# A decoder trunk on one core: low parts of the first layer's activations moved to 1280 bytes behind the high ones, raw weights in four buffers of 512 KB

## The chip, the cores and the metric

The kernel runs on one core of one Trainium2 chip. The metric is the device time of one execution in microseconds; for a single core that is the core's own time. A comparison takes the median of several runs.

## What is computed

The reference is a decoder trunk of two layers on 16 meta tokens and 256 input tokens (272 rows of 2048 features, float32). Cut to what matters:

```
h = concat(meta_tokens, x)                                    # 272 x 2048
# layer 0
q, k, v, f = split(rms_norm(h, g) @ fox_w_in)                 # 2048 x (3*2048 + 16)
h += forgetting_attention(q, k, v, cumsum(log_sigmoid(f + b))) @ fox_w_o
h += square(relu(rms_norm(h, g) @ w_up[0])) @ w_down[0]       # 2048 x 8192 x 2048
# layer 1
k, v = split(rms_norm(h, g_kv) @ w_kv)                        # 2048 x 4096
h += stick_breaking_attention(rms_norm(h, g) @ sb_w_q, k, v) @ sb_w_o
h += square(relu(rms_norm(h, g) @ w_up[1])) @ w_down[1]
return rms_norm(h, g)[16:]                                    # 256 x 2048
```

The work is in the products with the weight matrices, 384 MB of float32 in all, each read once.

## The kernel before, in words

Activations are kept feature-major: 16 chunks of 128 features on the partitions, with the tokens along the row. Every large product is made by `gemm_group` (L158): it makes 512 output features, four accumulators of 128 features, over all 16 chunks. There are 96 groups: 12 for q, k and v, 4 for the first output projection, 32 for the first MLP, 8 for the shared k and v, 4 for q of the second layer, 4 for its output projection, 32 for its MLP.

**The split.** A float32 factor is carried as a high part of type `float32r` and a low part, the rest that the high part leaves out. A product is hi x hi + hi x lo + lo x hi. For the weights the split is done in the group: a raw tile `raw` lands by DMA (L176), ACT copies it to `whi` (L185) and DVE subtracts to get `wlo` (L186), two chunks (half of a block of four chunks) at a time. For the activations a `Split` (L106) holds a tile of 16 rows, one for each chunk, with a row of `XROW` = 576 words; 16 words are left free at its head (`XHI`), then come `n` words of high part and, right behind, `n` words of low part. `n` is the number of tokens: 272 in the first layer and for the shared k and v (`t0` = 0), 256 (`S`) in the rest of the second (`t0` = 16).

**The matmuls.** With `pairs` off (n = 272) each chunk and accumulator gets three: whi with hi (L208), whi with lo (L209), wlo with hi (L210), 272 columns each. The weight is loaded anew for each. With `pairs` on (n = 256) there are two: whi with hi and lo together, 512 columns (L205), as both lie next to each other (`self.both`, L114), and wlo with hi, 256 columns (L206). The names in the profile: x_a, x_o, x_m, x_u and x_kv are `Split` tiles, so the 272-column lines with x_a are the projections q, k and v, with x_o the output projection, with x_m the up and with x_u the down products.

**Buffers.** Raw weights have three buffers of four chunks (1 MB, 8 KB in each partition), filled by one DMA each, except in the very first group, where x is loaded along with the weights and the pieces are 1, 2, 2 and 4 chunks (L172). `whi` and `wlo` have three buffers of two chunks each. Two `Split` tiles alternate.

**The order.** The program is written in the order of the groups; a scheduler with a timeline of its own reorders instructions of each engine a little and places the waits. All raw loads are issued by SP in the order of the program: a load waits until ACT and DVE have split what was in its buffer. ACT's split waits in turn until PE is done with a `whi` buffer. In a group, blocks 0 to 2 are run half by half (both chunks of a half for one accumulator after the other), block 3 accumulator by accumulator over all four chunks (L191 to L195); then each accumulator is evacuated by `evac`.

Of the kernel before, what the change touches and what calls it, by code (L numbers as in the profile page):

```python
# [9 lines left out]
F32 = mybir.dt.float32  # L10
# [5 lines left out]
P = 128  # L16
# [3 lines left out]
S = 256  # L20
# [2 lines left out]
BIG = 1.0e30  # L23
QSCALE = 1.0 / math.sqrt(P)
N_FF = 4
XROW = 576
XHI = 16

G_A0, G_M0, G_KV, G_A1, G_M1, G_FIN = range(6)

# [2 lines left out]
def yoco_kernel(ctx: ExitStack, tc: tile.TileContext, hT_in, gains, b_f, w_f, w_qkv0, w_o0, w_up, w_dn,  # L33
                w_kv, w_q1, w_o1, outT):
    nc = tc.nc

    const = ctx.enter_context(tc.tile_pool(name="const", bufs=1))
    wraw = ctx.enter_context(tc.tile_pool(name="wraw", bufs=3))

    align = ctx.enter_context(tc.tile_pool(name="align", bufs=1))  # L40
    wspl = ctx.enter_context(tc.tile_pool(name="wspl", bufs=3))
# [64 lines left out]
    class Split:  # L106


        def __init__(self, label, t0):
            n = T - t0  # L110
            self.t0 = t0
            rows = xs.tile([P, NC, XROW], F32R, tag="x", name=f"x_{label}")
            self.hi, self.lo = rows[:, :, XHI:XHI + n], rows[:, :, XHI + n:XHI + 2 * n]
            self.both = rows[:, :, XHI:XHI + 2 * n]  # L114

    def split_chunk(sp, gi, c):
# [41 lines left out]
    def gemm_group(wblk, sp, t0, evac, before={}, after={}, load_x=None, pairs=False):  # L158

        uid[0] += 1
        u = uid[0]
        accs = [pacc.tile([P, 512], F32, tag="acc", name=f"acc_{u}_{m}") for m in range(4)]
        n = T - t0
        for kb in range(4):
            raw = wraw.tile([P, 4, 512], F32, tag="raw", name=f"raw_{u}_{kb}")
            src_w = wblk[kb].rearrange("p (k c) -> p k c", k=4)
            if kb in before:  # L170
                before[kb]()
            piece = 4 if load_x is None else (1, 2, 2, 4)[kb]  # L172
            for k0 in range(0, 4, piece):
                if load_x is not None:
                    load_x(range(4 * kb + k0, 4 * kb + k0 + piece))
                nc.sync.dma_start(raw[:, k0:k0 + piece], src_w[:, k0:k0 + piece])  # L176
            piece = min(piece, 2)
            parts = []
            for hf in range(2):
                whi = wspl.tile([P, 2, 512], F32R, tag="whi", name=f"whi_{u}_{kb}_{hf}")  # L180
                wlo = wspl.tile([P, 2, 512], F32R, tag="wlo", name=f"wlo_{u}_{kb}_{hf}")
                for o in range(0, 2, piece):
                    src = raw[:, 2 * hf + o:2 * hf + o + piece, :]
                    hp, lp = whi[:, o:o + piece], wlo[:, o:o + piece]
                    on_act = nc.scalar.activation(hp, src, AF.Copy)  # L185
                    on_dve = nc.vector.tensor_tensor(out=lp, in0=src, in1=hp.bitcast(F32), op=ALU.subtract)  # L186
                parts.append((whi, wlo))
            if kb in after:
                with tc.issue_after(on_act.ins), tc.issue_after(on_dve.ins):
                    after[kb]()  # L190
            order = [(kc, m) for hf in range(2) for m in range(4) for kc in range(2 * hf, 2 * hf + 2)]  # L191
            if load_x is not None and kb == 0:
                order = [(kc, m) for kc in range(4) for m in range(4)]
            if kb == 3:
                order = [(kc, m) for m in range(4) for kc in range(4)]  # L195
            for kc, m in order:
                whi, wlo = parts[kc // 2]
                k = 4 * kb + kc
                wh = whi[:, kc % 2, m * P:(m + 1) * P]
                wl = wlo[:, kc % 2, m * P:(m + 1) * P]  # L200
                first = kb == 0 and kc == 0
                last = kb == 3 and kc == 3
                hi, lo = sp.hi[:, k], sp.lo[:, k]
                if pairs:
                    nc.tensor.matmul(accs[m], wh, sp.both[:, k], start=first, stop=False)  # L205
                    nc.tensor.matmul(accs[m][:, :n], wl, hi, start=False, stop=last)  # L206
                else:
                    nc.tensor.matmul(accs[m][:, :n], wh, hi, start=first, stop=False)  # L208
                    nc.tensor.matmul(accs[m][:, :n], wh, lo, start=False, stop=False)  # L209
                    nc.tensor.matmul(accs[m][:, :n], wl, hi, start=False, stop=last)  # L210
                if last:
                    evac(m, [accs[m][:, :n]] + ([accs[m][:, n:]] if pairs else []))
# [18 lines left out]
    def load_x(chunks):  # L231
        c0, n = chunks[0], len(chunks)
        nc.sync.dma_start(hT[:, c0:c0 + n, :], hT_in[:, c0:c0 + n, :])
        for c in chunks:
            split_chunk(xa, G_A0, c)
# [73 lines left out]
    for g in range(4):  # L309
# [11 lines left out]
        if g == 0:  # L321
            gemm_group(w_qkv0[0], xa, 0, evac_q, after={kb: (lambda kb=kb: first_norm(kb)) for kb in range(4)}, load_x=load_x)
            forget_gates(box["rstd"])
        else:
            gemm_group(w_qkv0[3 * g], xa, 0, evac_q)
# [4 lines left out]
        def decays(j):  # L330

            for i, (o, n) in enumerate(((0, 144), (144, T))):
                nc.vector.scalar_tensor_tensor(out=s[:, j, o:o + n], in0=fk[:, j, :n],
                                               scalar=fq_sb[:, i, 4 * g + j:4 * g + j + 1],
                                               in1=maskA[:, o:o + n], op0=ALU.subtract, op1=ALU.add)

        gemm_group(w_qkv0[3 * g + 1], xa, 0, lambda m, acc: evac_kv(m, acc, kT),
                   after={j: (lambda j=j: decays(j)) for j in range(4)})

# [261 lines left out]
    for b in range(2):  # L601
        nc.tensor.matmul(pr[:, b * P:(b + 1) * P], rs[:, b:b + 1].to_broadcast([P, P]), ident, start=True, stop=True)
    ob = xs.tile([P, NC, XROW], F32, tag="x", name="ob")
    for c in range(0, NC, 2):
# [54 lines left out]
```

## Time and profile before

| what | us |
|---|---|
| median of 3 runs | 2360.26 (2360.25 to 2360.53) |
| profiled execution, its own time | 2360.9 |
| span of that profile | 2359.2 |
| PE busy (matmuls) | 2340.6 |
| PEld busy (weight loads) | 2207.3 |
| DVE busy | 1343.8 |
| ACT busy | 1057.9 |
| mean granted TensorE clock | 0.998 |

The profile is one execution; its span runs from the first to the last instruction, and the execution's own time has 1.7 us around it. PE and PEld are two rows of one engine: a weight load runs beside the matmul before it, and a matmul's end is modelled and lies beyond the start of the next one. So durations of neighbours overlap, and what one matmul costs is the distance from its start to the next start. In a row of a group, `x1024 | 293.4, 289 | 0.0` means 1024 instructions, 293.4 us in which at least one of them was busy, 289 ns mean duration of one, and 0.0 us of idle time of the engine before them. In the view of one line, `284/289/289` is the minimum, median and maximum duration in ns. In a row of windows, the bounds come first, then the length, then for each engine its busy time with the count, then the clock, the DMA engines' share and GB/s.

### The profile page before, as it was taken

The numbers are of one execution on the slowest core, as the hardware profiler recorded it, in microseconds if no ns is written. First come the engines' busy times: TensorE is split into PE (matmuls) and PEld (weight loads), VectorE is DVE, ScalarE is ACT, GpSimd is POOL, SyncE is SP. The second block draws the span as 40 slices with busy tenths as digits, with TensorE's granted clock in tenths as the row PEclk, the third lists the DMA queues.
The fourth block names the chain that finished last, engine by engine and source line by source line (L and its number), as shares of the span: only waits on it lengthen the run. The fifth ranks groups of instructions, "written<-read, shape, count | busy, mean of one in ns | idle before, by whom it ended". The sixth has DMA issues, their size and how long they took to land.

```text
span 2359.2 us, 39072 instructions
## 1 busy us (share of the span) xinstructions
PE 2340.6 (99%) x16478; PEld 2207.3 (94%) x16478; DVE 1343.8 (57%) x1917; ACT 1057.9 (45%) x1473; POOL 35.2 (1%) x62
## 2 busy tenths in 40 slices
PE   8999999999999999999999999999999999999998
PEld 8999999999999999999998999988888888888887
DVE  7565555655455455445566555566555655655665
ACT  5443344543344344334445444445543543543544
POOL 0000000000000000000000000000000000000000
PEclk9999999999999999999999999999999999999999
DMA  6444444454545445544445444344545545455453
GB/s 231 147 166 171 154 160 163 176 181 168 189 163 185 173 179 179 179 179 172 179 168 197 155 147 145 143 177 180 184 177 193 194 181 197 171 188 195 178 196 125
DMA packets 60863, 411.92 MB, mean 175 GB/s; under 512 B 7040, under 2 KB 9744, under 8 KB 11920
## 3 DMA queue, kind: packets, MB, share of 16 engines
q1 hardware_dynamic: 59632, 407.05, 47.6%
q8 instruction: 129, 2.11, 0.3%
q10 hardware_dynamic: 1056, 2.38, 0.3%
q14 instruction: 46, 0.38, 0.0%
HBM read 407.29 MB, written 2.11 MB: 174 GB/s over the span
## 4 chain that ended last, share of the span: by engine, by line
PE 99%; DVE 0%; ACT 0%; DMA 0%; issue 0%; SPq 0%; DVEq 0%
PE acc L205 25%; PE acc L208 19%; PE acc L209 19%; PE acc L210 19%; PE acc L206 13%; PE ps L345 0%; PE pza L521 0%; PE pv L287 0%; PE po L406 0%; PE po L407 0%; PE po L560 0%; DVE ob L605 0%; PE po L561 0%; PE pzb L522 0%; DMA raw<-w_qkv 0%; PE po L408 0%
## 5 line engine op out<-in xcount | busy, mean ns | idle before, releaser
L186 DVE TENSOR_TENSOR wlo<-raw,whi 128x1024 fp32r<-128x1024 f32 (+1 forms) x770 | 932.0, 1220 | 764.3 <-ACT whi L185 761.2
L185 ACT ACTIVATE whi<-raw 128x1024 fp32r<-128x1024 f32 (+1 forms) x770 | 803.0, 1055 | 1071.4 <-PE acc L209 675.7
L205 PE MATMUL acc<-x_m,whi 128*128 128x512 f32 x1024 | 343.1, 394 | 0.5 <-DVE relu L223 0.5
L205 PE MATMUL acc<-x_u,whi 128*128 128x512 f32 x1024 | 343.0, 394 | 0.0
L208 PE MATMUL acc<-x_m,whi 128*128 128x272 f32 x1024 | 293.4, 289 | 0.0
L208 PE MATMUL acc<-x_u,whi 128*128 128x272 f32 x1024 | 293.2, 289 | 0.0
L209 PE MATMUL acc<-x_m,whi 128*128 128x272 f32 x1024 | 290.4, 286 | 0.0
L209 PE MATMUL acc<-x_u,whi 128*128 128x272 f32 x1024 | 290.3, 286 | 0.0
L210 PE MATMUL acc<-x_u,wlo 128*128 128x272 f32 x1024 | 280.7, 284 | 0.0
L210 PE MATMUL acc<-x_m,wlo 128*128 128x272 f32 x1024 | 280.7, 284 | 0.0
L206 PE MATMUL acc<-x_m,wlo 128*128 128x256 f32 x1024 | 252.7, 282 | 0.0
L206 PE MATMUL acc<-x_u,wlo 128*128 128x256 f32 x1024 | 251.4, 281 | 0.0
L208 PE MATMUL acc<-x_a,whi 128*128 128x272 f32 x768 | 222.9, 294 | 6.3 <-ACT whi L185 6.3
L209 PE MATMUL acc<-x_a,whi 128*128 128x272 f32 x768 | 221.9, 292 | 0.0
L205 PEld LDWEIGHTS acc<-x_u,whi 128*128 128x128 f32 x1024 | 185.4, 188 | 30.6
L205 PEld LDWEIGHTS acc<-x_m,whi 128*128 128x128 f32 x1024 | 185.0, 188 | 30.2 <-DVE relu L223 0.9
L210 PE MATMUL acc<-x_a,wlo 128*128 128x272 f32 x768 | 212.3, 288 | 0.0
L206 PEld LDWEIGHTS acc<-x_m,wlo 128*128 128x128 f32 x1024 | 192.2, 188 | 19.6 <-DVE wlo L186 4.8
L206 PEld LDWEIGHTS acc<-x_u,wlo 128*128 128x128 f32 x1024 | 192.3, 188 | 16.1 <-DVE wlo L186 1.5
L208 PEld LDWEIGHTS acc<-x_m,whi 128*128 128x128 f32 x1024 | 192.5, 188 | 0.0
L208 PEld LDWEIGHTS acc<-x_u,whi 128*128 128x128 f32 x1024 | 192.5, 188 | 0.0
L209 PEld LDWEIGHTS acc<-x_m,whi 128*128 128x128 f32 x1024 | 192.3, 188 | 0.0
(242 smaller groups left out, 3604.2 us busy)
## 6 DMA issues: line engine op xcount, KB each, us to landing
raw<-w_up SPq DMA_DIRECT2D x128, 1024.0 KB, 4.8
raw<-w_dn SPq DMA_DIRECT2D x128, 1024.0 KB, 4.8
raw<-w_qkv SPq DMA_DIRECT2D x45, 1024.0 KB, 4.7
raw<-w_o SPq DMA_DIRECT2D x32, 1024.0 KB, 4.7
raw<-w_kv SPq DMA_DIRECT2D x32, 1024.0 KB, 4.8
raw<-w_q SPq DMA_DIRECT2D x16, 1024.0 KB, 4.8
fk<-f_dram ACTq DMA_DIRECT2D x4, 544.0 KB, 5.3
raw<-w_qkv SPq DMA_DIRECT2D x4, 512.0 KB, 7.1
```

The costliest lines, as they stand in the source:

```text
L185: on_act = nc.scalar.activation(hp, src, AF.Copy)
L186: on_dve = nc.vector.tensor_tensor(out=lp, in0=src, in1=hp.bitcast(F32), op=ALU.subtract)
L205: nc.tensor.matmul(accs[m], wh, sp.both[:, k], start=first, stop=False)
L206: nc.tensor.matmul(accs[m][:, :n], wl, hi, start=False, stop=last)
L208: nc.tensor.matmul(accs[m][:, :n], wh, hi, start=first, stop=False)
L209: nc.tensor.matmul(accs[m][:, :n], wh, lo, start=False, stop=False)
L210: nc.tensor.matmul(accs[m][:, :n], wl, hi, start=False, stop=last)
```

## The change

Rows of the `Split` tiles become 640 words (2560 bytes) long. For n = 272 the low part starts at word 336 instead of word 288, which is 320 words (1280 bytes) behind the start of the high part instead of 272 words (1088 bytes); between both lie 48 unused words. For n = 256 the low part stays right behind the high part, 1024 bytes on. The two tiles need 8192 bytes a partition more.

The raw weights get four buffers of two chunks (512 KB, 4 KB in each partition) instead of three of four, 8192 bytes a partition less. Each block of four chunks is now loaded by two DMAs, one for each half, and each half has a tile of its own. In the first group the pieces are 1, 2, 2 and 2 chunks.

```diff
-XROW = 576
+XROW = 640
 XHI = 16
+XLO = 336
...
-    wraw = ctx.enter_context(tc.tile_pool(name="wraw", bufs=3))
+    wraw = ctx.enter_context(tc.tile_pool(name="wraw", bufs=4))
...
-            self.hi, self.lo = rows[:, :, XHI:XHI + n], rows[:, :, XHI + n:XHI + 2 * n]
+            lo = XHI + n if n == S else XLO
+            self.hi, self.lo = rows[:, :, XHI:XHI + n], rows[:, :, lo:lo + n]
             self.both = rows[:, :, XHI:XHI + 2 * n]
...
-            raw = wraw.tile([P, 4, 512], F32, tag="raw", name=f"raw_{u}_{kb}")
             src_w = wblk[kb].rearrange("p (k c) -> p k c", k=4)
             if kb in before:
                 before[kb]()
-            piece = 4 if load_x is None else (1, 2, 2, 4)[kb]
+            piece = 1 if load_x is not None and kb == 0 else 2
+            raws = [wraw.tile([P, 2, 512], F32, tag="raw", name=f"raw_{u}_{kb}_{hf}") for hf in range(2)]
             for k0 in range(0, 4, piece):
                 if load_x is not None:
                     load_x(range(4 * kb + k0, 4 * kb + k0 + piece))
-                nc.sync.dma_start(raw[:, k0:k0 + piece], src_w[:, k0:k0 + piece])
-            piece = min(piece, 2)
+                nc.sync.dma_start(raws[k0 // 2][:, k0 % 2:k0 % 2 + piece], src_w[:, k0:k0 + piece])
             parts = []
             for hf in range(2):
...
-                    src = raw[:, 2 * hf + o:2 * hf + o + piece, :]
+                    src = raws[hf][:, o:o + piece, :]
```

## The prediction

> **What bounds the kernel now.** I read the profile's page first, in the order span, busy engines, clock, chain of work that ended last. PE is busy for 2340.6 of 2359.2 us at a full granted clock, and PE is 99% of the chain; nearly all of that chain stands on five lines, L205, L206, L208, L209 and L210, the matmuls of `gemm_group`. So the time is a count of matmuls times their spacing, and a change counts if it alters that spacing or makes PE wait.
>
> ```profile
> span 2359.2 us, 39072 instructions
> PE 2340.6 (99%) x16478; PEld 2207.3 (94%) x16478; DVE 1343.8 (57%) x1917; ACT 1057.9 (45%) x1473; POOL 35.2 (1%) x62
> PEclk9999999999999999999999999999999999999999
> PE 99%; DVE 0%; ACT 0%; DMA 0%; issue 0%; SPq 0%; DVEq 0%
> PE acc L205 25%; PE acc L208 19%; PE acc L209 19%; PE acc L210 19%; PE acc L206 13%; PE ps L345 0%; PE pza L521 0%; PE pv L287 0%; PE po L406 0%; PE po L407 0%; PE po L560 0%; DVE ob L605 0%; PE po L561 0%; PE pzb L522 0%; DMA raw<-w_qkv 0%; PE po L408 0%
> ```
>
> Next the groups by line: the counts and the mean duration of one. The lines L208 (hi), L209 (lo), L210 (hi again, with the low part of the weight) form triples of 272 columns; L205 and L206 are the pairs of 512 and 256 columns.
>
> ```profile
> L205 PE MATMUL acc<-x_m,whi 128*128 128x512 f32 x1024 | 343.1, 394 | 0.5 <-DVE relu L223 0.5
> L208 PE MATMUL acc<-x_m,whi 128*128 128x272 f32 x1024 | 293.4, 289 | 0.0
> L208 PE MATMUL acc<-x_u,whi 128*128 128x272 f32 x1024 | 293.2, 289 | 0.0
> L206 PE MATMUL acc<-x_m,wlo 128*128 128x256 f32 x1024 | 252.7, 282 | 0.0
> L206 PE MATMUL acc<-x_u,wlo 128*128 128x256 f32 x1024 | 251.4, 281 | 0.0
> L208 PE MATMUL acc<-x_a,whi 128*128 128x272 f32 x768 | 222.9, 294 | 6.3 <-ACT whi L185 6.3
> ...
> L208 PE MATMUL acc<-x_kv,whi 128*128 128x272 f32 x512 | 146.6, 289 | 0.0
> L208 PE MATMUL acc<-x_o,whi 128*128 128x272 f32 x256 | 73.4, 289 | 0.0
> ```
>
> The triples number 1024 + 1024 + 768 + 512 + 256 = 3584. A matmul overlaps the next, so its duration is not its cost; the spacing is. Two windows count starts: 700 us of triples, then 400 us of pairs.
>
> ```profile
> 500.00:1200.00 700.00, 536.97 (x1876) 352.44 (x1875) 1.00 0.49 177
> 1900.00:2300.00 400.00, 380.13 (x1138) 205.50 (x1137) 1.00 0.51 187
> ```
>
> A triple takes 700 / 1876 = 373.1 ns, 124.4 each; a pair takes 400 / 1138 = 351.5 ns. Now the row that decides, the durations of the three lines (minimum/median/maximum):
>
> ```profile
> L208 PE MATMUL acc<-x_u,whi x1006: 284/289/289, 537.9 to 1199.8; 128*128 128x272 f32 x168
> ...
> L209 PE MATMUL acc<-x_u,whi x1006: 286/286/286, 538.0 to 1199.9; 128*128 128x272 f32 x168
> ...
> L210 PE MATMUL acc<-x_u,wlo x1005: 284/284/289, 538.1 to 1199.7; 128*128 128x272 f32 x168
> ```
>
> There are only three values. L208 and L210 read the same bytes, yet one is mostly 289 and the other mostly 284. The timeline tells which is which.
>
> ```profile
> 699.79 0.28 PE L210 MATMUL acc<-x_m,wlo 128*128 128x272 f32 x1
> 699.92 0.29 PE L208 MATMUL acc<-x_m,whi 128*128 128x272 f32 x1
> 700.04 0.29 PE L209 MATMUL acc<-x_m,whi 128*128 128x272 f32 x1
> 700.17 0.28 PE L208 MATMUL acc<-x_m,whi 128*128 128x272 f32 x1
> 700.29 0.29 PE L209 MATMUL acc<-x_m,whi 128*128 128x272 f32 x1
> 700.41 0.28 PE L210 MATMUL acc<-x_m,wlo 128*128 128x272 f32 x1
> ```
>
> L208 lasts 0.29 behind L210 (hi behind hi) and 0.28 behind L209 (hi behind lo), with L209 behind it both times; the two pairs begun by these L208 take 0.25 and 0.24 us. So a matmul's cost goes by where it and the one ahead of it start reading: hi behind hi 289, lo behind hi 286, hi behind lo 284. Their mean 286.3 less the spacing 124.4 gives 161.9 of overlap; the spacings are about 127, 124 and 122 ns.
>
> **Part one: where lo starts.** In the built program the x tiles start at a multiple of 256 bytes in both kernels, and rows of 2304 and 2560 bytes are 9 and 10 times 256. Hi starts 64 bytes behind such a multiple. Lo starts 1088 bytes on, 128 behind a multiple, before; 1280 bytes on, so 64 behind a multiple as hi does, after. The stationary tiles move by 8192 bytes and keep their residues. Hence after the change each matmul of a triple stands behind one of its own kind, which is what hi behind hi is now. I have three estimates of that spacing.
>
> First, the durations: 289 less 161.9 is 127.1; three are 381.3, 8.2 more than 373.1.
>
> Second, the start, where the first group runs equal lines in a row:
>
> ```profile
> 10.98 1.04 PE L210 MATMUL acc<-x_a,wlo 128*128 128x272 f32 x4
> 11.86 0.66 PE L208 MATMUL acc<-x_a,whi 128*128 128x272 f32 x4
> 12.35 0.55 PE L209 MATMUL acc<-x_a,whi 128*128 128x272 f32 x3
> 12.73 0.55 PE L210 MATMUL acc<-x_a,wlo 128*128 128x272 f32 x3
> 13.12 0.29 PE L209 MATMUL acc<-x_a,whi 128*128 128x272 f32 x1
> ```
>
> From 11.86 to 13.12 there are ten spacings in 1260 ns: eight of like behind like, lo behind lo among them, one lo behind hi and one hi behind lo. A triple is one of each, 373.1; so seven like ones are 1260 - 373.1 = 886.9, one is 126.7, and three are 380.1: 7.0 more.
>
> Third, the pairs, in which lo follows hi without a gap and every read starts 64 behind a multiple: durations 394 and 282, less (394 + 282 - 351.5) / 2 = 162.2, give 231.8 and 119.8. One column costs (231.8 - 119.8) / 256 = 0.4375 ns, 16 more 7.0; 272 columns would take 126.8, three of them 380.4: 7.3 more.
>
> Ends are modelled in the first and the third, and the second rests on ten matmuls rounded to 10 ns, so I take the lower side, **6.5 ns a triple**. 3584 x 6.5 = 23.3 us, all on the path, since PE waits for nothing there (idle 0.0 in the rows). Bounds: 3584 x 8.2 = 29 us above; below, nothing or a gain by the rivals.
>
> A rule of the Trainium skill speaks against any such term: "TensorE: Matmul & The Clock Gate", section "Back-to-back issue gap", gives the gap as N / 2.4 + 2.5 ns, 115.8 for 272 columns, with no word of where a read starts. The trace differs, with 124.4 on the mean and three values for one size. By the rule the term would be zero, the second rival below.
>
> The rows of the pairs are also moved, from 2304 to 2560 bytes; their starts keep their residue of 256, so I take 0. The L206 of the two tiles differ by 1 ns (282 and 281) though all else is alike; that much on the 2048 pairs of these tiles is 2 us either way.
>
> **Part two: the raw weights.** Each load of 1 MB becomes two of 512 KB in four buffers: 2 MB ahead in place of 3. SP issues 381 loads more (four in each of 95 groups, one in the first), with little else to do: it has 0% of the chain. A buffer is free when ACT (L185) and DVE (L186) have split it, so the load for half h waits for DVE's split of half h - 4 and must land before ACT's split of h. The shortest such distance in the trace is at the start of a group in the second layer:
>
> ```profile
> 1857.35 3.50 DVE L186 TENSOR_TENSOR wlo<-raw,whi 128x1024 fp32r<-128x1024 f32 x3 [1.63 <-ACT whi L185]
> ...
> 1863.45 1.06 ACT L185 ACTIVATE whi<-raw 128x1024 fp32r<-128x1024 f32 x1 [1.72 <-PE acc L205]
> ```
>
> The first of the three splits ends near 1858.57 and the split four halves on begins at 1863.45: 4.9 us. What the loads take:
>
> ```profile
> raw<-w_up SPq DMA_DIRECT2D x128, 1024.0 KB, 4.8
> raw<-w_qkv SPq DMA_DIRECT2D x4, 512.0 KB, 7.1
> ```
>
> The whole 1 MB lands in 4.8 us in the steady part, so a half of it lands in time; the 7.1 belongs to the crowded start. ACT there waits for PE, and PE has another split half in hand. I take 0. The Trainium skill speaks against it too: "SBUF — State Buffer", section "The DMA setup-cost knee", wants the largest single transfer, as each pays some 2 us. By its fit, an estimate, 512 KB take 3.2 us and 1 MB 4.4; the trace has 4.8 for the latter. This would not make the halves late.
>
> At the start the halves matter more. The load of the fourth block goes out at 12.27 before; after, its halves wait for the splits of the third and fourth half:
>
> ```profile
> 12.27 45.54 SPq L176 DMA_DIRECT2D raw<-w_qkv  x8
> ...
> 13.96 1.23 DVE L186 TENSOR_TENSOR wlo<-raw,whi 128x1024 fp32r<-128x1024 f32 x1 [0.26 <-ACT whi L185]
> ...
> 15.92 1.22 DVE L186 TENSOR_TENSOR wlo<-raw,whi 128x1024 fp32r<-128x1024 f32 x1
> ...
> 23.66 1.99 ACT L185 ACTIVATE whi<-raw 128x1024 fp32r<-128x1024 f32 x2
> ```
>
> So they go out at 15.2 and 17.1, up to 4.9 us later, and are split at 23.66, 6.5 us behind the second; the DMA engines have earlier loads to move meanwhile. I take 0, between a gain of 1 (the first half no longer waits for the second) and a loss of 4.9. The order on PE, DVE and ACT differs in a few dozen rows, nearly all in the first three groups; also 0.
>
> **Sum.** 2360.9 for the profiled execution (2359.2 of span and 1.7 around it) + 23.3 = 2384.2. The median of the three runs is 2360.3, 0.6 lower: 2383.6, a little under 1% slower.
>
> **The rivals.**
> *Like starts are what is cheap.* If hi behind hi is dear only because chunk and weight change there, and it is the different start of lo that costs, every matmul would go at the pace of hi behind lo: 122.1 ns, 3 x 122.1 = 366.3, 6.8 less, 3584 x 6.8 = 24 us faster, 2336. It decides from the point where like behind like falls below 124.4. For it: no row shows hi behind a lo with hi's start. Against it: in the run of ten, equal starts, some with the chunk unchanged, cost 126.7.
> *Only the columns count.* A pair costs 351.5 / 768 = 0.458 ns a column, a triple 373.1 / 816 = 0.457. If the durations only share out a fixed sum, nothing changes: 2360, give or take 3. Against it: the two pairs of 0.25 and 0.24 us, with equal columns.
> *The halves come late.* If a half took the 7.1 us of the start, each of the 16 up groups of the second layer would lose 7.1 - 4.9 = 2.2 us, 35 us on top of the forecast: 2419. The 4.8 us for twice the bytes speak against it.
> *It doesn't do what it says.* Another base of the tiles could undo the alignment; the built addresses exclude that.
>
> **How the numbers follow.** Forecast 0.67, late halves 0.03, columns alone 0.18, like starts cheap 0.12. Slower by over 0.2% (4.7 us, about what a measurement of this kernel can tell from no change) is 0.70, within it 0.18, faster 0.12. The range must take in the second rival, since the forecast alone is under 0.8: from 2357 to 2391, the forecast with 29 us and 2 more at the top. The forecast's own range is 2376 to 2391.
>
> **What would show it.** If right, L208, L209 and L210 all last 289 in the rows, whatever stands ahead, a window of triples gives 126.5 ns a start, L205 and L206 keep 394 and 282, and PE has no new idle time. All at 284 makes the first rival; unequal durations with 124.4 the second; idle PE behind ACT's split with a DMA named, the third. A changed time in the pairs, or a row stride that matters beyond 256 bytes, would make the prediction wrong in another way.

## The result, and the profile after

The changed kernel takes 2382.71 us (median of 4 runs, 2382.05 to 2383.3) where the kernel before takes 2360.4 beside it (4 runs, 2360.25 to 2360.92). The ratio is 1.0093, with a 95% interval of 1.008 to 1.0106: slower by 22.3 us, where 23.3 were forecast.

The page of the profile after, the lines that answer to those of before. All line numbers of `gemm_group` are one higher: L209 is hi, L210 lo, L211 wlo with hi, L206 and L207 the pairs.

```profile
span 2381.6 us, 40038 instructions
PE 2363.1 (99%) x16478; PEld 2229.9 (94%) x16478; DVE 1344.3 (56%) x1917; ACT 1057.5 (44%) x1473; POOL 33.4 (1%) x62
...
PE 99%; DVE 0%; ACT 0%; DMA 0%; issue 0%; SPq 0%; DVEq 0%
...
L206 PE MATMUL acc<-x_m,whi 128*128 128x512 f32 x1024 | 343.2, 394 | 0.5 <-DVE relu L224 0.5
...
L209 PE MATMUL acc<-x_m,whi 128*128 128x272 f32 x1024 | 293.9, 289 | 0.0
...
L210 PE MATMUL acc<-x_m,whi 128*128 128x272 f32 x1024 | 293.7, 289 | 0.0
...
L211 PE MATMUL acc<-x_m,wlo 128*128 128x272 f32 x1024 | 285.5, 289 | 0.0
L207 PE MATMUL acc<-x_m,wlo 128*128 128x256 f32 x1024 | 252.6, 282 | 0.0
```

The span grew by 22.4 us and PE's busy time by 22.5, with the same 16478 matmuls and the same clock. The pairs kept 394 and 282. The view of each line shows that the three values of before have become one:

```profile
L209 PE MATMUL acc<-x_u,whi x955: 289/289/289, 545.5 to 1199.8; 128*128 128x272 f32 x191
...
L210 PE MATMUL acc<-x_u,whi x955: 289/289/289, 545.6 to 1200.0; 128*128 128x272 f32 x191
...
L211 PE MATMUL acc<-x_u,wlo x954: 289/289/289, 545.7 to 1199.7; 128*128 128x272 f32 x191
```

Minimum, median and maximum are all 289. The two windows, triples first:

```profile
500.00:1200.00 700.00, 528.06 (x1842) 345.62 (x1841) 1.00 0.53 174
...
1900.00:2300.00 400.00, 380.05 (x1137) 205.38 (x1136) 1.00 0.56 187
```

A triple takes 700 / 1842 = 380.0 ns, 6.9 more than before; a pair 400 / 1137 = 351.8, as before (one start more or less in a window is 0.2 and 0.3 ns). PE's waits are those of before, some 10 us in all, and the loads of half the size land, by their medians, inside the 4.9 us that were needed:

```profile
PE acc L209 <- ACT whi L186: 6.4, 1, 6.4
PE pr_fin L603 <- DVE fin L600: 1.5, 1, 1.5
```

```profile
raw<-w_up SPq DMA_DIRECT2D x256, 512.0 KB, 4.5
...
raw<-w_o SPq DMA_DIRECT2D x64, 512.0 KB, 3.8
```

So the whole loss stands in the triples. Summed from each start to the next over both traces they grew by 22.3 us, which is 6.2 ns each on the mean of all 3584. It is 6.6 to 6.7 ns in the up and down groups, where the window lies (its 6.9 carries one start more or less in both counts), 6.4 in the output projection, 5.6 in the shared k and v and 5.5 in q, k and v. What was open is why, and whether it was the reason that the prediction gave: a cost for each pair of starts, with like behind like the dearest.

### The profile page after: what moved, and what is told of

Read it like the earlier page. It is cut to its first block, busy times and chain, and to the rows that moved or that the text cites. A ratio compares the mean times of both kernels' runs of the same rounds, so it can differ in the third digit from the quotient of the medians.

```text
span 2381.6 us, 40038 instructions
## 1 busy us (share of the span) xinstructions
PE 2363.1 (99%) x16478; PEld 2229.9 (94%) x16478; DVE 1344.3 (56%) x1917; ACT 1057.5 (44%) x1473; POOL 33.4 (1%) x62
## 4 chain that ended last, share of the span: by engine, by line
PE 99%; DVE 0%; ACT 0%; DMA 0%; issue 0%; SPq 0%; DVEq 0%
PE acc L206 25%; PE acc L211 19%; PE acc L210 19%; PE acc L209 19%; PE acc L207 13%; PE ps L346 0%; PE pza L522 0%; PE pv L288 0%; PE po L407 0%; PE po L408 0%; PE po L561 0%; DVE ob L606 0%; DMA raw<-w_qkv 0%; PE po L562 0%; PE pzb L523 0%; PE po L409 0%
## 5 line engine op out<-in xcount | busy, mean ns | idle before, releaser
L206 PE MATMUL acc<-x_m,whi 128*128 128x512 f32 x1024 | 343.2, 394 | 0.5 <-DVE relu L224 0.5
L206 PE MATMUL acc<-x_u,whi 128*128 128x512 f32 x1024 | 343.0, 394 | 0.0
L209 PE MATMUL acc<-x_m,whi 128*128 128x272 f32 x1024 | 293.9, 289 | 0.0
L209 PE MATMUL acc<-x_u,whi 128*128 128x272 f32 x1024 | 293.7, 289 | 0.0
L210 PE MATMUL acc<-x_m,whi 128*128 128x272 f32 x1024 | 293.7, 289 | 0.0
L210 PE MATMUL acc<-x_u,whi 128*128 128x272 f32 x1024 | 293.7, 289 | 0.0
L211 PE MATMUL acc<-x_u,wlo 128*128 128x272 f32 x1024 | 285.5, 289 | 0.0
L211 PE MATMUL acc<-x_m,wlo 128*128 128x272 f32 x1024 | 285.5, 289 | 0.0
L207 PE MATMUL acc<-x_m,wlo 128*128 128x256 f32 x1024 | 252.6, 282 | 0.0
L207 PE MATMUL acc<-x_u,wlo 128*128 128x256 f32 x1024 | 251.5, 281 | 0.0
L209 PE MATMUL acc<-x_a,whi 128*128 128x272 f32 x768 | 223.1, 294 | 6.4 <-ACT whi L186 6.4
L210 PE MATMUL acc<-x_a,whi 128*128 128x272 f32 x768 | 223.3, 294 | 0.0
L211 PE MATMUL acc<-x_a,wlo 128*128 128x272 f32 x768 | 214.5, 292 | 0.0
L206 PEld LDWEIGHTS acc<-x_u,whi 128*128 128x128 f32 x1024 | 185.5, 188 | 30.5
L206 PEld LDWEIGHTS acc<-x_m,whi 128*128 128x128 f32 x1024 | 184.9, 188 | 30.4 <-DVE relu L224 0.9
L207 PEld LDWEIGHTS acc<-x_m,wlo 128*128 128x128 f32 x1024 | 192.4, 188 | 19.5 <-DVE wlo L187 4.7
L207 PEld LDWEIGHTS acc<-x_u,wlo 128*128 128x128 f32 x1024 | 192.3, 188 | 16.1 <-DVE wlo L187 1.6
L209 PEld LDWEIGHTS acc<-x_m,whi 128*128 128x128 f32 x1024 | 192.2, 188 | 0.0
L209 PEld LDWEIGHTS acc<-x_u,whi 128*128 128x128 f32 x1024 | 192.2, 188 | 0.0
L210 PEld LDWEIGHTS acc<-x_m,whi 128*128 128x128 f32 x1024 | 192.2, 188 | 0.0
```

## The experiments

Each was timed beside the kernel before, and a ratio below is to that kernel. "At 64" means 64 bytes behind a multiple of 256. Where nothing else is said, the stationary tiles (the `whi` and `wlo` that a weight load reads) start at 0 in this sense, hi starts at 64 and the second layer is as before.

**1. The raw buffers alone.** Edit of the changed kernel:

```diff
-XROW = 640
+XROW = 576
...
-            lo = XHI + n if n == S else XLO
+            lo = XHI + n
```

> The raw weights in four buffers of 512 KB alone; the activations keep rows of 2304 bytes with lo 1088 bytes behind hi. Theory A (the cost of a matmul goes by where it and the one ahead of it start reading, modulo 256 bytes; the loads cost nothing): 2360, within 3 us of before; L208-kind rows 289, lo rows 286, wlo rows 284. Theory B (the halved loads make the loss, by late splits or more DMA traffic): 2375 to 2385.

2360.76 us against 2361.0, ratio 0.9999 (0.9991 to 1.0008). The three lines have their old durations, and the window of triples counts the same 1876 starts as before:

```profile
500.00:1200.00 700.00, 536.97 (x1876) 352.44 (x1876) 1.00 0.55 177
```

The halved loads raise the DMA engines' share in it from 0.49 to 0.55 and cost nothing. Theory B is out.

**2. Only the start of lo undone.** Rows of 2560 bytes and the new buffers stay:

```diff
-            lo = XHI + n if n == S else XLO
+            lo = XHI + n
```

> Rows of 2560 bytes and the four raw buffers, but lo 1088 bytes behind hi as before: of the change, only the start of lo is undone. Theory A: 2360, within 3 us of before, durations 289, 286 and 284 again. Theory B (loads) or C (the row pitch of 2560 bytes costs, because each chunk starts at the same place modulo 512): 2375 to 2385, and under C the pairs of the second layer are dearer too.

2360.73 us, ratio 0.9999 (0.999 to 1.0008), again 1876 triples, durations with medians of 289, 286 and 284. The row pitch costs nothing either: the start of lo is the whole change.

**3 and 4. Lo at two other places.**

```diff
-XLO = 336
+XLO = 304      # run 3: lo at 192
...
+XLO = 320      # run 4: lo at 0
```

> As the changed kernel, but lo starts 1152 bytes behind hi, 192 behind a multiple of 256 (hi at 64). Theory A: hi behind hi stays at 126.6 ns; lo behind hi and hi behind lo are new, each between the 121.7 and 126.6 seen so far, so 2348 to 2383, and both alike, as the distance is 128 both ways. Theory D (what counts is only that lo shares hi's start): as before the change, 2360.

> As the changed kernel, but lo starts 1216 bytes behind hi, on a multiple of 256 (hi at 64). Theory A by the distance of the starts: lo stands 64 ahead of hi modulo 256, so lo behind hi costs what hi behind lo did (121.7, duration 284), hi behind lo what lo behind hi did (125.2, duration 286), hi behind hi 126.6: 2360 again, with the durations of the second and third line swapped. If lo's own place counts and not the distance, another sum.

Run 3 takes 2361.37 us, ratio 1.0002 (0.9993 to 1.0011), run 4 2368.54, ratio 1.0032 (1.0019 to 1.0044). Run 4 misses theory A's 2360. It also speaks against D, since lo no longer shares hi's start and 7.5 us stay lost. Run 3 agrees with A's wide range and with D alike. The durations of run 3 tell more than its time:

```profile
L209 PE MATMUL acc<-x_u,whi x1003: 286/288/290, 538.5 to 1199.9; 128*128 128x272 f32 x168
...
L210 PE MATMUL acc<-x_u,whi x1002: 286/286/288, 538.7 to 1199.7; 128*128 128x272 f32 x167
...
L211 PE MATMUL acc<-x_u,wlo x1002: 287/288/290, 538.8 to 1199.8; 128*128 128x272 f32 x167
```

L209 is still hi behind hi, both at 64, most of the time; its median is 288 here, not 289, with a spread that was not there. Theory A held that cost fixed.

**5. Another row pitch, so that hi behind hi is no longer alike.** Edit of the kernel before:

```diff
+XROW_A = 560
...
-            rows = xs.tile([P, NC, XROW], F32R, tag="x", name=f"x_{label}")
+            pitch = XROW if n == S else XROW_A
+            rows = xs.tile([P, NC * XROW], F32R, tag="x", name=f"x_{label}")
+            rows = rows[:, :NC * pitch].rearrange("p (c w) -> p c w", c=NC)
```

> The kernel before with rows of 2240 bytes where 272 columns are read (no gap behind lo), so that the next chunk's hi starts 64 bytes earlier modulo 256 and hi behind hi is no longer like behind like. The second layer keeps its rows of 2304. Theory A (a fixed cost for each pair of starts): lo behind hi and hi behind lo stay at 125.2 and 121.7, hi behind hi becomes 121.7 upward and 125.2 back down, 123.5 on the mean instead of 126.6: 3584 x 3.1 = 11 us less, 2349. Theory E (only triples whose three starts are all alike pay more, anything else takes about 373.5): 2358 to 2363.

2367.61 us, ratio 1.0028 (1.0018 to 1.0039): 18.6 us above what theory A gave, and outside what E gave. The cheap transitions of before didn't come along; all three lines, L211 to L213 in this kernel, have a median of 288:

```profile
L211 PE MATMUL acc<-x_u,whi x991: 283/288/290, 539.7 to 1199.7; 128*128 128x272 f32 x199
...
L212 PE MATMUL acc<-x_u,whi x991: 283/288/296, 539.8 to 1199.8; 128*128 128x272 f32 x199
...
L213 PE MATMUL acc<-x_u,wlo x991: 283/288/292, 540.0 to 1199.9; 128*128 128x272 f32 x199
```

Theories A and E fall as general rules.

**6. All alike, at 0.** Edit of the changed kernel:

```diff
-            lo = XHI + n if n == S else XLO
-            self.hi, self.lo = rows[:, :, XHI:XHI + n], rows[:, :, lo:lo + n]
+            h0, lo = (XHI, XHI + n) if n == S else (0, 320)
+            self.hi, self.lo = rows[:, :, h0:h0 + n], rows[:, :, lo:lo + n]
```

> As the changed kernel, but in the 272-column tiles hi starts on a multiple of 256 (word 0) and lo 1280 bytes behind it, also on one: again all alike, at another place. The second layer is as before. Theories A and E: 126.6 ns each, 2383. Theory F (the place itself counts, for instance against the stationary tiles, which start on multiples of 256): another time, by the spread of what has been seen 2340 to 2400.

2369.97 us, ratio 1.0038 (1.0025 to 1.0052), 12.7 us below the changed kernel. The place counts, then, with the distances between reads the same.

**7 and 8. 256 columns instead of 272,** in the 14 inner chunks of each product, in the changed kernel (run 7) and in the one before (run 8). A read is then 1024 bytes long, four times 256:

```diff
                 hi, lo = sp.hi[:, k], sp.lo[:, k]
+                if not pairs and not (first or last):
+                    n, hi, lo = 256, hi[:, :256], lo[:, :256]
+                else:
+                    n = T - t0
```

> The changed kernel, with the 14 inner chunks of each 272-column product reading 256 columns (the last 16 tokens' share of these chunks is left out). 9408 matmuls lose 16 columns, some 6.7 ns each, 63 us: 2383 - 63 = 2320 if the start alone counts (theories A, E). If it is the distance from the end of one read to the start of the next (theory G), like behind like with 256 columns is a distance of 0 modulo 256, as lo behind hi was (125.2 at 272): 118.5 each, 2307.

> The kernel before with the same 256 columns in the 14 inner chunks. Starts alone (A, E): 2360 - 63 = 2298, 22 us less than the changed kernel with 256 columns. Distance from end to start (G): hi behind hi 0, lo behind hi 64, hi behind lo 192 modulo 256; the last was the dearest (126.6 at 272), so less of a difference between the two, under 12 us.

2297.38 us for the changed kernel, 2300.76 for the one before (ratios to the kernel before 0.9732, 0.9719 to 0.9746, and 0.9745, 0.9731 to 0.9758). The changed kernel's 22 us are gone, and in the first MLP a triple takes 600 / 1684 = 356.3 ns in run 7 and 600 / 1685 = 356.1 in run 8, the same within one start:

```profile
550.00:1150.00 600.00, 464.88 (x1684) 316.28 (x1684) 1.00 0.57 185
...
550.00:1150.00 600.00, 464.98 (x1685) 318.48 (x1685) 1.00 0.53 185
```

So the length of the reads decides along with their starts. Run 8 lies within 3 us of the 2298 that starts alone gave, but run 7 lies 23 us below the 2320 that they gave for it. That speaks for theory G's small difference, but G's 2307 for run 7 misses by 10 us too.

**9 and 10. Against the stationary tiles.** `pad` is a tile of 128 bytes ahead of the stationary and the activation tiles; halved, it moves both down by 64 bytes (run 9). Run 10 moves hi and lo back up by 16 words, so that the stationary tiles alone have moved:

```diff
-    pad = align.tile([P, 32], F32, name="pad")
+    pad = align.tile([P, 16], F32, name="pad")     # runs 9 and 10
...
-XHI = 16
+XHI = 32                                           # run 10 alone
...
-XLO = 336
+XLO = 352                                          # run 10 alone
```

> The changed kernel with the stationary tiles and the activation tiles both moved 64 bytes down (a pad ahead of them halved): hi and lo start on multiples of 256, the stationary tiles 192 behind one; the distance between the two streams stays 64. Theory R (what counts is how a read lies against the weight load that runs beside it): all spacings as in the changed kernel, 126.6 for each of the three, and the second layer unchanged, 2383. Theory F (the place of the read itself counts): the three lines at 125.4 as in the run with all starts on multiples of 256, 2370, with some change in the second layer.

> The changed kernel with the stationary tiles alone moved 64 bytes down; hi and lo stay 64 behind a multiple of 256, so the distance to the stationary tiles grows from 64 to 128. Theory F: 126.6 for each of the three lines, 2383, the second layer as before. Theory R: other spacings, for the pairs of the second layer too; 2350 to 2400, no more than 1 us from 2383 only by chance.

Run 9 takes 2382.82 us, ratio 1.0096 (1.0081 to 1.0111), the changed kernel's time though hi and lo now start at 0, where run 6 took 2369.97. Its rows are those of the changed kernel:

```profile
L209 PE MATMUL acc<-x_u,whi x953: 289/289/289, 546.1 to 1199.7; 128*128 128x272 f32 x191
...
1900.00:2300.00 400.00, 379.84 (x1137) 205.42 (x1136) 1.00 0.56 187
```

Run 10 takes 2388.9 us, ratio 1.012 (1.0103 to 1.0137). Its triples count 1842 in the window, as in the changed kernel, but its pairs, whose own starts did not move, are dearer, 400 / 1130 = 354.0 ns:

```profile
500.00:1200.00 700.00, 529.15 (x1842) 346.71 (x1841) 1.00 0.53 174
...
1900.00:2300.00 400.00, 379.21 (x1130) 204.27 (x1129) 1.00 0.56 187
```

So it is not the place in memory that counts but how the reads lie against the weights that are loaded beside them (theory R): moved together, nothing changes; moved apart, something does. In run 10 that something is the time of the pairs; the triples keep their mean, though their durations now spread from 287 to 292 ns. Theory F missed both times, by 13 us in run 9 and by 6 in run 10.

One rival has its answer in the changed kernel's trace. ACT and DVE write `whi` and `wlo`, which moved as well, and it might be their writes that the reads must be clear of. But between 500 and 1190 us the distance from start to start is 126 or 127 ns, 126.7 on the mean, both while ACT or DVE is at work and while neither is.

**11 and 12. The two places left.** Run 11 is the changed kernel with both starts at 192, run 12 the kernel before with hi at 0 and lo at 128, each by the edit of run 6 with other numbers:

```diff
+            h0, lo = (XHI, XHI + n) if n == S else (48, 368)   # run 11
...
+            h0, lo = (XHI, XHI + n) if n == S else (0, 288)    # run 12
```

> As the changed kernel, but in the 272-column tiles hi starts 192 bytes behind a multiple of 256 and lo 1280 bytes on, so both lie 192 behind the stationary tiles' start modulo 256; the second layer is as before. Seen so far for equal starts: 125.4 ns at 0, 126.6 at 64 and at 128. If equal starts are dear at each place: 125.4 to 126.6 again, 2369 to 2383. If only the places 64 and 128 are dear: 124.5 or less, 2360 or below.

> The kernel before with hi of the 272-column tiles on a multiple of 256 (word 0) and lo 128 behind one (word 288); the second layer and the raw buffers are as before. Equal starts at 0 were cheaper (125.4) than at 64 (126.6), and the mixed triples with hi at 64 and lo at 128, 192 or 0 took 373.5, 373.7 and 375.8 ns. If a gain of hi's place adds to the mixing, a triple falls by up to 3.6 ns, 13 us: 2348. If only the mixing counts: 2360, within 3.

Run 11 takes **2349.86 us**, ratio 0.9953 (0.994 to 0.9965): the fastest of all, 11.0 us under the kernel before and 32.9 under the changed one, with the same rows of 2560 bytes, the same 1280 bytes between hi and lo and the same buffers. Its last triple of the first MLP begins at 1196.8 us, so the window is closed at 1196 here. A triple takes 696 / 1882 = 369.8 ns, 123.3 each:

```profile
500.00:1196.00 696.00, 534.10 (x1882) 354.40 (x1882) 1.00 0.55 178
```

Run 12 takes 2361.3 us, ratio 1.0001 (0.9992 to 1.001). Set beside run 6 it settles theory A. In both, L209 is in most cases hi behind hi, each at 0, with the stationary tiles at the same places; run 6 first, then run 12:

```profile
L209 PE MATMUL acc<-x_u,whi x985: 284/288/291, 541.2 to 1199.9; 128*128 128x272 f32 x197
```

```profile
L209 PE MATMUL acc<-x_u,whi x1006: 284/284/288, 538.0 to 1199.7; 128*128 128x272 f32 x168
```

The same pair of starts has a median of 288 in one and 284 in the other. From start to next start, between 500 and 1190 us, it costs 125.4 ns in run 6 and 122.1 in run 12. What a matmul costs depends on more than its own start and that of the one ahead.

All fixed placements of 272 columns together, by the starts of hi and lo against the stationary tiles (modulo 256), with the count of triples in the same 700 us (696 for run 11). Run 5, whose starts differ from chunk to chunk, has 1865 triples; runs 1 and 2 have the placement of before.

| hi, lo | kernel | triples | ns a triple | us |
|---|---|---|---|---|
| 64, 128 | before | 1876 | 373.1 | 2360.4 |
| 64, 64 | changed | 1842 | 380.0 | 2382.7 |
| 64, 64 | run 9 | 1843 | 379.8 | 2382.8 |
| 64, 192 | run 3 | 1874 | 373.5 | 2361.4 |
| 64, 0 | run 4 | 1864 | 375.5 | 2368.5 |
| 0, 0 | run 6 | 1863 | 375.7 | 2370.0 |
| 0, 128 | run 12 | 1876 | 373.1 | 2361.3 |
| 128, 128 | run 10 | 1842 | 380.0 | 2388.9 (pairs dearer too) |
| 192, 192 | run 11 | 1882 in 696 us | 369.8 | 2349.9 |

## Why the prediction was right

*What bounds the kernel.* Right: the loss is PE's own spacing, with no new wait.

*The term.* 6.5 ns a triple were taken, 23.3 us; the total gives 6.2 on the mean of all triples, the window 6.9. The step that carried it was to find the order to come, hi at 64 behind hi at 64 with 272 columns and the same stationary places, already present in the trace as every third matmul. Its 289 came true for all three lines. Measured from start to next start between 500 and 1190 us of the trace before, hi behind hi stands 126.7 ns, lo behind hi 125.0 and hi behind lo 121.7; three times the first is 380.0, which is what a triple takes after the change. The prediction's first estimate had 127, 124 and 122 in their place, because it took one overlap for all three durations, and so came out 1.3 ns too high. The run of ten at the start had given 380.1, but its single spacings lie between 121 and 131 ns, so that it comes this close is luck. The 6.5 was taken below all three estimates (7.0 to 8.2) as a caution: the up and down groups went above it, the projections below, and that the two nearly cancel had not been foreseen.

*The loads, the pitch, the start.* All three were put at 0. Run 1 has the loads at 0, within 2 us either way; run 2 pitch and loads together. The load of 512 KB takes 3.8 to 4.5 us, under the 4.8 of 1 MB that had served as a bound, and PE has no new wait for a split. It is over the 3.2 us estimated from the Trainium skill's "SBUF — State Buffer", section "The DMA setup-cost knee"; the measurement decides, and the sum had not used the estimate. At the start three matmuls fewer fit into the first 30 us, kernel before first:

```profile
0.00:30.00 30.00, 23.72 (x170) 23.72 (x171) 25.61 (x46) 22.93 (x45) 5.00 (x22) 1.00 0.84 305
```

```profile
0.00:30.00 30.00, 23.62 (x167) 23.62 (x168) 25.19 (x45) 22.45 (x44) 5.14 (x22) 1.00 0.82 289
```

That would be some 0.4 us, inside the bounds given, but it can't be put down to the halves: runs 1 and 2, which have them too, have 169 and 176 there.

*The rivals.* "Only the columns count" is out: equal columns took from 369.8 to 380.0 ns a triple. So is, for this kernel, the formula beside it from the Trainium skill's "TensorE: Matmul & The Clock Gate", section "Back-to-back issue gap", in which the columns alone set the gap. The section gives it for an isolated matmul and says that in a stream of weight loads and matmuls both set the spacing, which the prediction left out. "Like starts are what is cheap" was wrong at 64 and right at 192: its point of decision, under 124.4 ns, is met by 123.3. The evidence against it, the run of ten, held for the places 64 and 128 and not for like starts as such.

*What was too simple.* The prediction read the three durations as a cost for each pair of starts. That gives the changed kernel's time but not those of runs 4, 5, 6 and 11, and run 12 beside run 6 contradicts it. The forecast escaped this because the change puts lo at the very place that hi already had; with both at 0 or at 192 the same reasoning would have given 2383 again, where 2370.0 and 2349.9 were measured. Shown is that the placement of lo against hi makes the whole change (run 2), that the stationary tiles' place belongs to it (runs 9 and 10), and that the length of the reads does too (runs 7 and 8). How the three make 370 or 380 ns stays open; the table is a table of results, not a law. Starts between multiples of 64 bytes were not tried, nor the second layer's pairs at other places than those of the prediction and of runs 9 and 10.

## What to carry to other kernels

Where matmuls stand without a gap, compare the durations of lines that do the same work: 284 beside 289 on the same bytes was the whole sign of an effect that made this kernel from 0.5% faster (run 11) to 0.9% slower (the change). If the order to come already occurs somewhere in the trace, its row prices the change better than a rule does; but a row prices that one case, and a rule drawn from three rows (like behind like is dear) failed at the next place. Equal placement of two operands is no aim in itself: trying the few places gave the fastest kernel here.

## What the runs showed of the hardware that was not expected

With all starts equal, a matmul of 272 columns of float32r takes from 123.3 ns (starts 192 bytes behind those of the stationary tiles, modulo 256) to 126.7 (64 and 128 behind), with 125.2 at 0. Moving the reads and the stationary tiles together changes nothing (2382.8 beside 2382.7 us); moving the stationary tiles alone by 64 bytes made the pairs of the second layer 2.2 ns dearer (354.0 beside 351.8). With reads of 256 columns in 14 of 16 chunks the two placements that differ by 22 us at 272 differ by 3.4 us, the other way round, while in the first MLP their triples take the same within one start (356.3 and 356.1 ns).
